# Pacing of attention and projections in the first layer: ratio 2.3 from a running base, without a lead

## The chip, the cores and the metric

The kernel runs on one core of a Trainium2 chip. The metric is the device time of one launch in microseconds (us); the time before is the median of three runs. The profiled execution is a further run with the hardware profiler on; its rows name the engines PE (TensorE matmul), PEld (TensorE weight load, overlapping PE), DVE (VectorE), ACT (ScalarE), POOL (GpSimd) and SP (SyncE, which issues the DMAs).

## The reference

A trunk of two layers on 1024 tokens of width 1024; each computes `x <- x + W_out(mixer(RMSNorm(x)) * silu(z))`. Layer 1 is a native sparse attention and is not touched by the change. Layer 0 is forgetting attention with 16 heads of 64:

```python
q, k, v, f, z = split(h @ w_in)
c = cumsum(log_sigmoid(f + b_f), axis=1)
logits = q @ k.T * HEAD_DIM ** -0.5 + c[query] - c[key]     # causal
o = softmax(logits) @ v
return (o * silu(z)) @ w_out
```

## The kernel before

**Two streams and a merge.** Layer 0 is written as two generators whose instructions are laid into one order by the function `merge`. `fox_main` is the attention, `fox_fill` the filling work, above all projections. Each generator yields the cost of what it has just emitted (a number, in the planner's nanoseconds), or a function that must become true before it goes on. `merge` takes one payment after another from `main`, adds it to `paid`, and after each lets `fill` run until `done`, the sum of the filling work, reaches `base + ratio * (paid + off)`. If `main` gives a function that isn't true yet, `fill` runs alone until it is. If `fill` itself gives such a function, fill is refused and attention goes on without it. A scheduler then places the instructions on the engines' queues, by priority in the written order; each engine runs its queue in order.

**The filling work.** For each of the 8 pairs of heads: `fox_k`, `fox_v`, `fox_q`, `fox_z`, each two halves of 512 tokens, each half 8 steps of three 128x512 matmuls (`project` through `mm3`, lines 132 to 134, cost 650 a step). `fox_k` of pair p >= 2 waits until pair p-2 is scored, `fox_v` until its products are done (the K and V tiles have two sets). Weights come by DMA into one staging tile (`load_w`, line 124), are cast on DVE (line 127), and POOL subtracts the cast for the low part (line 128). In pair 7, `load_wout` brings the output weights in two halves (ACT casts, line 525, POOL subtracts, line 526, eight each per half). After pair 7 comes `out_start`: products of the output projection for token tiles 4, 5 and 6. For tiles 4 and 5 the first four of their eight row blocks (16 steps) need pairs 0 to 3 only; the next three (12 steps) need pair 6; tile 6 (14 steps) waits until all scores are emitted.

**The attention.** A `FoxDuo` is two query tiles of one head: duo p.j.x is pair p (0 to 7), head j (0, 1) of the pair, x (0 to 3); there are 64. `score` makes the bias block `Bd` on POOL (line 563), multiplies queries with keys (lines 574 and 575) into one of three PSUM banks `S`, adds the bias and takes the running minimum on DVE (line 583), the exponential on ACT (line 592), splits the result into high and low half-precision parts (`hl`, ACT line 593, DVE line 594), and SP issues transposing DMAs into `pT` (line 595). `pv`, emitted two duos later, multiplies by V into a PSUM bank `O` (lines 608 and 609); `finish` reads it back on DVE (`ot`, line 620, and `o`, line 622). At the end of a pair the outputs are transposed (`pto`, line 630) and stored. `fox_main` emits the score of duo n, a payment, then the products of duo n-2, a second payment. The costs are `2 * max(n * 0.42, 107)` for each block of n columns scored and `85 * nk` for the products over nk key tiles. Eight duos before the end `fox_main` yields the tuple `(LAST,)`, by which `merge` sets the ratio anew and starts `paid` and `base` from that point.

**PSUM.** The banks `A` (three) hold projections, `O` and, from `out_start` on, output products.

Of the kernel before, what the change touches and what calls it, by code (L numbers as in the profile page):

```python
# [39 lines left out]
def tile_fox_nsa(ctx, tc, a, out):  # L40
# [156 lines left out]
    def merge(main, fill, ratio, off=0.0, until=None, rebase=False):  # L197

        done, paid, base = 0.0, 0.0, None

        def step():
            if blocked:
                if not blocked[0]():
                    return None
                blocked.pop()
            try:
                c = next(fill)
            except StopIteration:  # L210
                return None
            if callable(c):
                blocked.append(c)
                return 0.0
            return c

        for c in main:
            if callable(c):
                while not c():
                    n = step()  # L220
                    assert n is not None
                    done += n
                continue
            if isinstance(c, tuple):
                ratio, off, paid, base = c[0], 0.0, 0.0, done
                continue
            if base is None:
                base = done
            if rebase:
                base = max(base, done - ratio * (paid + off))  # L230
            paid += c
            while done < base + ratio * (paid + off):
                n = step()
                if n is None:
                    break
                done += n
        while not (until and until()) and step() is not None:
            pass
# [17 lines left out]
    def next_w(take=True):  # L256
        while len(wq) < 2 and fox_order:
            wq.append(wsec(*fox_order.pop(0)))
        return wq.pop(0) if take else None
# [53 lines left out]
    def fox_k(p):  # L313
        KH = [sa.tile([P, S], F32R, tag="KH", bufs=4, name=f"KH_{p}_{j}") for j in range(2)]
        KL = [sa.tile([P, S], F32R, tag="KL", bufs=4, name=f"KL_{p}_{j}") for j in range(2)]
        w = next_w() if p else wq.pop(0)
        for half in range(2):
            ts = slice(half * 512, half * 512 + 512)
            pt = ps_a(f"k{p}_{half}")
            yield from project(w, hT, half, pt)  # L320
            for j in range(2):
                r, o = rows[j], rows[1 - j]
                A.copy(KH[j][r, ts], pt[r, :])
                V.tensor_tensor(KL[j][r, ts], pt[r, :], f(KH[j][r, ts]), OP.subtract)
                dma(f(KH[j][o, ts]), f(KH[j][r, ts]))
                dma(f(KL[j][o, ts]), f(KL[j][r, ts]))
            yield 0
        ready["k", p] = KH, KL
# [57 lines left out]
    def fox_v(p):  # L386


        w = next_w()
        v = sa.tile([P, 2, 2, 4, P], F16, tag="v", bufs=2, name=f"v_{p}")  # L390
        sc = sa.tile([P, 4], F32, tag="vsc", bufs=3, name=f"vsc_{p}")
        vT = []
        for half in range(2):
            pt = ps_a(f"v{p}_{half}")
            yield from project(w, hT, half, pt)
            vT.append(f(sa.tile([P, 512], F32R, tag="Q", bufs=8, name=f"vT_{p}_{half}")))
            A.activation(vT[half], pt, AF.Abs, accum_out=sc[:, half:half + 1])
            A.copy(vT[half], pt)
        V.tensor_scalar(sc[:, 0:1], sc[:, 0:1], sc[:, 1:2], 2.0 ** -100, OP.max, OP.max)
        e, r = (sc[:, i:i + 1].bitcast(I32) for i in (2, 3))  # L400
        V.tensor_scalar(e, sc[:, 0:1].bitcast(I32), 0x7F800000, None, OP.bitwise_and)
        V.tensor_scalar(r, e, 0x7F800000, None, OP.bitwise_xor)
        V.tensor_scalar(sc[:, 3:4], sc[:, 3:4], 2.0 ** 13, None, OP.mult)
        V.tensor_scalar(sc[:, 2:3], sc[:, 2:3], 2.0 ** -15 / UP, None, OP.mult)
        for half in range(2):
            vs = sa.tile([P, 2, 512], F16, tag="vs", bufs=2, name=f"vs_{p}_{half}")
            A.activation(vs[:, 0], vT[half], AF.Copy, scale=sc[:, 3:4])
            V.scalar_tensor_tensor(vs[:, 1], vT[half], sc[:, 3:4], vs[:, 0], OP.mult, OP.subtract)
            nc.sync.dma_start_transpose(v[:, half].rearrange("p c t d -> p (c t) d"), vs.rearrange("p c t -> p (c t)"))
        ready["v", p] = v, sc[:, 2:3]  # L410

    def fox_q(p, w, halves=(1, 0)):
        Q = ready.setdefault(("qt", p), {})
        for half in halves:
            pt = ps_a(f"q{p}_{half}")
            yield from project(w, hT, half, pt)
            for j in range(2):
                Q[half, j] = q = sa.tile([P, 512], F32R, tag="Q", bufs=8, name=f"Q_{p}_{half}_{j}")
                r, o = rows[j], rows[1 - j]
                A.activation(q[r, :], pt[r, :], AF.Copy, scale=-SCALE)  # L420
                V.scalar_tensor_tensor(q[o, :], pt[r, :], -SCALE, f(q[r, :]), OP.mult, OP.subtract)
            ready["q", p, half] = Q

    def fox_z(p, w, halves=(1, 0)):
        zs = ready.setdefault(("zt", p), {})
        for half in halves:
            pt = ps_a(f"z{p}_{half}")
            yield from project(w, hT, half, pt)
            zs[half] = z = sb[0].tile([P, 512], F32, tag="z", bufs=4, name=f"z_{p}_{half}")
            silu2(z, pt)  # L430
            ready["z", p, half] = zs

    def fox_fill():
        for p in range(8):
            if p >= 2:
                yield lambda p=p: ("scored", p - 2) in ready
            yield from k0 if p == 0 else fox_k(p)
            if p == 0:
                for _ in range(11):
                    yield next(gate0)  # L440
            if p >= 2:
                yield lambda p=p: ("done", p - 2) in ready
            yield from fox_v(p)
            if p == 0:
                yield from gate0
                sb.append(tc.alloc_tile_pool(name="sb", bufs=2, reuse_waits="tile"))
            wo_copy(0, p)
            if p < 7:
                yield from fox_q(p, next_w())
                yield from fox_z(p, next_w())  # L450
            else:
                wq, wz = next_w(), next_w()
                for half in (1, 0):
                    yield from fox_q(p, wq, (half,))
                    yield from fox_z(p, wz, (half,))
                    yield from load_wout(hp, 0, half)
        yield from out_start()
# [55 lines left out]
    def wo_copy(i, k):  # L513
        dma(wD[i][k * P:(k + 1) * P, :], a[("fox_w_out", "nsa_w_out")[i]][k * P:(k + 1) * P, :])

    def load_wout(pool, i, half):

        hi, lo = (pool.tile([P, 4, D], F32R, tag=f"h{half}{x}", name=f"wo{i}_{half}_{x}") for x in range(2))
        for k in range(4):
            r = 4 * (1 - half) + k  # L520
            dma(f(lo[:, k, :]), wD[i][r * P:(r + 1) * P, :])
        for k in range(4):
            for c in range(2):
                cs = slice(c * 512, c * 512 + 512)
                A.copy(hi[:, k, cs], f(lo[:, k, cs]))
                G.tensor_tensor(lo[:, k, cs], f(lo[:, k, cs]), f(hi[:, k, cs]), OP.subtract)  # L526
            yield 200
        ready.setdefault("wout", []).append((hi, lo))


    PACE, LAST = 2.6, 2.6

    class FoxDuo:

# [113 lines left out]
    def fox_main():  # L648
        duos = [FoxDuo(p, j, x) for p in range(8) for j in range(2) for x in range(4)]
        for n in range(len(duos) + 2):  # L650
            if n == len(duos) - 8:
                yield (LAST,)
            if n < len(duos):
                yield from burst(duos[n].score(u) for u in (1, 0))
                if duos[n].j == 1 and duos[n].x == 3:
                    ready["scored", duos[n].p] = True
                    if duos[n].p == 7:
                        ready["scores"] = True
            if n >= 2:
                yield from burst(duos[n - 2].pv(u) for u in (0, 1))  # L660
                yield from duos[n - 2].finish()

    merge(fox_main(), fox_fill(), PACE, 5000)
    sb[0].release()
    sa.release()

# [725 lines left out]
```

## Time and profile before

| | |
|---|---|
| median of three runs | 1571.32 us (1570.53 to 1571.86) |
| the profiled execution | 1573.4 us, its span 1571.6 us |
| mean granted TensorE clock | 0.983 |
| PE / DVE / ACT / POOL busy | 95% / 71% / 56% / 35% of the span |
| layer 0's two streams | about 71 us to about 606 us |

The span runs from the first to the last instruction that the profile shows. Matmuls are pipelined and their ends are modelled, so a busy PE is not PE at its peak. In a row of the timeline the bracket gives the idle time of the engine just before the instruction and what released it. The granted clock is a mean over a stretch: 1.00 is TensorE's full 2.4 GHz, 0.50 the lower level of 1.2 GHz.

### The profile page before, as it was taken

How to read it: one execution, taken by the hardware profiler on the slowest of the kernel's cores; microseconds unless marked ns; L12 is line 12 of the kernel's file. 1: busy time of each engine (PE TensorE's matmuls, PEld its weight loads, DVE VectorE, ACT ScalarE, POOL GpSimd, SP SyncE). 2: the span in 40 equal slices, each digit the busy share in tenths (PEclk: the TensorE clock that was granted, in tenths of full speed). 3: DMA queues.
4: the chain of work that ended last, by engine and by line, in shares of the span. 5: the costliest groups of instructions: out<-in, count | busy, mean ns of one | idle time of the engine just before them, and what ended most of it. 6: DMA issues, size and time to landing. Idle time of an engine off the chain costs nothing.

```text
span 1571.6 us, 26098 instructions
## 1 busy us (share of the span) xinstructions
PE 1488.9 (95%) x8536; PEld 1245.3 (79%) x8536; DVE 1110.7 (71%) x2880; ACT 873.6 (56%) x2145; POOL 555.6 (35%) x596
## 2 busy tenths in 40 slices
PE   6999999999999787999999989999999999999898
PEld 4888888888777566878888777788888888888786
DVE  6568878788686855456464776888888888887433
ACT  5455655555555643233133544777787788787522
POOL 1222222232223400034242232546555556556400
PEclk9999999999999878999999999999999999999999
DMA  7777787777677756332436555502312312212452
GB/s 259 234 144 163 161 165 150 165 161 160 148 153 171 165 119 208 115 119 90 141 120 186 188 188 174 188 28 82 122 53 69 122 41 68 75 55 81 141 161 94
DMA packets 253945, 213.14 MB, mean 136 GB/s; under 512 B 179632, under 2 KB 201008, under 8 KB 253552
## 3 DMA queue, kind: packets, MB, share of 16 engines
q1 hardware_dynamic: 253808, 211.46, 49.2%
q8 instruction: 68, 1.11, 0.3%
q14 instruction: 69, 0.57, 0.1%
HBM read 123.06 MB, written 46.20 MB: 108 GB/s over the span
## 4 chain that ended last, share of the span: by engine, by line
PE 52%; DVE 12%; ACT 7%; DMA 4%; issue 4%; POOL 1%; SPq 0%; POOLq 0%; DVEq 0%; ACTq 0%
PE ptp_n L1250 7%; PE S_n L1226 7%; PE O_n L1259 3%; PE O_n L1258 3%; PE y L134 3%; PE y L133 3%; PE y L132 3%; ACT cP L1033 2%; DVE hl L594 2%; ACT P L592 1%; PE nz L132 1%; PE nz L133 1%; PE nz L134 1%; DMA wo<-wD 1%; ACT P_n L1234 1%
## 5 line engine op out<-in xcount | busy, mean ns | idle before, releaser
L1238 POOL TENSOR_SCALAR P_n<-P_n,l_n,gates 128x640 f32<-128x640 f32 (+7 forms) x256 | 200.9, 791 | 176.2 <-DVE l_n L1236 143.5
L145 DVE TENSOR_TENSOR ptl_n<-ptp_n,pth_n 128x512 fp32r<-128x512 f32 (+1 forms) x272 | 181.3, 672 | 35.3 <-ACT pth_n L144 31.6
L1234 ACT ACTIVATE P_n<-P_n,m_n 128x640 f32<-128x640 f32 (+7 forms) x256 | 188.5, 737 | 23.8 <-DVE m_n L1233 22.0
L144 ACT CAST pth_n<-ptp_n 128x512 fp32r<-128x512 f32 (+1 forms) x272 | 153.7, 568 | 73.5 <-PE ptp_n L1250 72.1
L592 ACT ACTIVATE P<-P,m 128x512 f32<-128x512 f32 (+1 forms) x192 | 116.8, 609 | 126.6 <-DVE m L583 125.9
L1226 PE MATMUL S_n<-nk,nq 128*128 128x320 f32 (+5 forms) x768 | 171.7, 333 | 0.2 <-DVE m_n L1233 0.2
L1250 PE MATMUL ptp_n<-ident,P_n 128*128 128x128 f32 x1056 | 166.9, 275 | 4.6 <-DVE ptl_n L145 2.9
L563 POOL TENSOR_TENSOR Bd<-B,tri 128x128 f32<-128x128 f32 x128 | 61.4, 491 | 250.6 <-DVE m L583 237.3
L1250 PEld LDWEIGHTS ptp_n<-ident,P_n 128*128 128x128 f32 x1056 | 124.6, 140 | 30.9 <-DVE ptl_n L145 8.1
L1258 PE MATMUL O_n<-pth_n,nv 128*128 128x512 f32 (+3 forms) x384 | 140.1, 369 | 0.8 <-DVE ot_n L1269 0.3
L1226 PEld LDWEIGHTS S_n<-nk,nq 128*128 128x128 f32 x768 | 128.0, 188 | 15.3 <-DVE m_n L1233 1.9
L594 DVE SCALAR_TENSOR_TENSOR hl<-P,hl 128x512 f16<-128x512 f32 (+1 forms) x192 | 125.7, 670 | 19.5 <-ACT hl L593 18.1
L1259 PE MATMUL O_n<-ptl_n,nv 128*128 128x512 f32 (+3 forms) x384 | 120.7, 338 | 0.1
L1233 DVE CUSTOM_DVE_ANT_0 P_n<-S_n,wmask 128x128 f32<-128x128 f32 (+1 forms) x192 | 113.3, 591 | 9.0 <-PE S_n L1226 4.7
L132 PE MATMUL y<-wo,ohi 128*128 128x512 f32 x240 | 97.1, 405 | 8.7 <-ACT ohi L688 4.6
L133 PE MATMUL y<-wo,ohi 128*128 128x512 f32 x240 | 96.6, 403 | 3.7 <-POOL wo L526 3.7
L134 PE MATMUL y<-wo,olo 128*128 128x512 f32 x240 | 95.8, 401 | 2.0 <-DVE olo L468 1.4
L593 ACT ACTIVATE hl<-P 128x512 f16<-128x512 f32 (+1 forms) x192 | 92.7, 513 | 3.4 <-DMA pT<-hl 1.7
L1258 PEld LDWEIGHTS O_n<-pth_n,nv 128*128 128x128 f32 x384 | 72.6, 189 | 6.9 <-DVE ot_n L1269 1.3
L574 PE MATMUL S<-KH,Q 128*128 128x512 f32 (+1 forms) x192 | 68.7, 372 | 8.0 <-DVE m L583 7.8
L1259 PEld LDWEIGHTS O_n<-ptl_n,nv 128*128 128x128 f32 x384 | 73.0, 190 | 2.2 <-DVE ptl_n L145 0.3
L608 PE MATMUL O<-v,pT 128*128 128x128 f16 x576 | 61.8, 226 | 8.3 <-DVE ot L620 4.7
(361 smaller groups left out, 4030.1 us busy)
## 6 DMA issues: line engine op xcount, KB each, us to landing
nq<-qD SPq DMA_DIRECT2D x64, 256.0 KB
B<-cD SPq DMA_DIRECT2D x16, 512.0 KB
wo<-wD SPq DMA_DIRECT2D x16, 512.0 KB
nq<-qD SPq DMA_DIRECT2D x64, 128.0 KB
of<-oF SPq DMA_DIRECT2D x12, 512.0 KB
x<-in_x_dram SPq DMA_DIRECT2D x8, 512.0 KB
wst_k<-in_fox_w_dram SPq DMA_DIRECT2D x8, 512.0 KB
wst_v<-in_fox_w_dram SPq DMA_DIRECT2D x8, 512.0 KB
```

The source lines that it names most:

```text
L132: T.matmul(ps, wh, mh, start=first, stop=False, **kw)
L133: T.matmul(ps, wh, ml, start=False, stop=False, **kw)
L134: T.matmul(ps, wl, mh, start=False, stop=last, **kw)
L144: A.copy(hi[:, 0:n], pt[:, 0:n])
L145: V.tensor_tensor(lo[:, 0:n], pt[:, 0:n], f(hi[:, 0:n]), OP.subtract)
L594: V.scalar_tensor_tensor(lo[:, cs], L[:, 0:n], UP, hi[:, cs], OP.mult, OP.subtract)
L1226: T.matmul(ps[:, b, 0:w], self.q[x][:, qi * P:(qi + 1) * P], k[:, k0 + b * w:k0 + b * w + w], start=(x == 0), stop=(x == 1))
L1234: A.activation(L, L, AF.Exp, bias=m, scale=-1.0, accum_out=lr[:, 0, qi:qi + 1])
L1238: G.tensor_scalar(L, L, lr[:, 1, qi:qi + 1], gates[:, i, x:x + 1], OP.mult, OP.mult)
L1250: T.transpose(pt[:, (x + i) * P:(x + i + 1) * P], L[:, kb * P - k0:(kb + 1) * P - k0], ident)
L1258: T.matmul(po[:, d], v, hi[:, c], start=(b == i == 0), stop=False)
L1259: T.matmul(po[:, d], v, lo[:, c], start=False, stop=(b == len(self.blocks) - 1 and i == len(pieces) - 1))
```

## The change

`PACE` becomes 2.3. The call for layer 0 loses the offset of 5000 and passes `rebase=True`, a branch of `merge` that the call of layer 1 already uses: ahead of each payment `base` is raised to `done - ratio * (paid + off)` if it lies below, so filling work that is ahead, because it ran alone or because its last step overshot, is not taken back later. `LAST` stays 2.6. No instruction is added or removed; only their order changes.

```diff
-    PACE, LAST = 2.6, 2.6
+    PACE, LAST = 2.3, 2.6
...
-    merge(fox_main(), fox_fill(), PACE, 5000)
+    merge(fox_main(), fox_fill(), PACE, rebase=True)
```

The lines of `merge` that this concerns:

```python
            if base is None:
                base = done
            if rebase:
                base = max(base, done - ratio * (paid + off))
            paid += c
            while done < base + ratio * (paid + off):
```

## Rows read from the trace of the kernel before

**Rows 1.** The page: busy us of each engine, share of the span, instructions.

```profile
PE 1488.9 (95%) x8536; PEld 1245.3 (79%) x8536; DVE 1110.7 (71%) x2880; ACT 873.6 (56%) x2145; POOL 555.6 (35%) x596
```

**Rows 2.** Windows: stretch, its length, PE, PEld, DVE, ACT, POOL busy, clock, DMA share, GB/s.

```profile
72.20:507.00 434.80, 428.40 (x2667) 351.75 (x2666) 333.63 (x996) 244.03 (x611) 127.05 (x144) 0.99 0.74 158
320.00:340.00 20.00, 20.00 (x134) 16.43 (x134) 18.20 (x54) 12.29 (x34) 6.53 (x8) 1.00 0.81 172
531.00:554.00 23.00, 14.46 (x112) 10.21 (x108) 19.25 (x70) 14.43 (x40) 4.24 (x9) 0.85 0.73 155
```

**Rows 3.** Timeline of PE in the opening: start, us, engine, line, output<-inputs.

```profile
72.24 0.40 PE L133 MATMUL z<-hT,whi_z 128*128 128x512 f32 x1
...
88.35 0.34 PE L574 MATMUL S<-KH,Q 128*128 128x384 f32 x1
...
95.92 0.23 PE L608 MATMUL O<-v,pT 128*128 128x128 f16 x1
```

**Rows 4.** Timeline of PE around the duos 4.1.3 and 5.0.1.

```profile
380.23 0.31 PE L574 MATMUL S<-KH,Q 128*128 128x128 f32 x1
...
381.47 0.23 PE L608 MATMUL O<-v,pT 128*128 128x128 f16 x1
...
383.18 0.50 PE L132 MATMUL k<-hT,whi_k 128*128 128x512 f32 x1 [0.77 <-DVE ot L620]
...
400.67 0.62 PE L132 MATMUL v<-hT,whi_v 128*128 128x512 f32 x1 [2.47 <-DVE ot L620]
```

**Rows 5.** Windows of DVE, lines 583, 594, 620, 622 in turn (34 duos).

```profile
100.00:369.00 269.00, 65.52 (x304) 1.00 0.77 163
...
100.00:369.00 269.00, 66.48 (x102) 1.00 0.77 163
...
100.00:369.00 269.00, 13.66 (x33) 1.00 0.77 163
...
100.00:369.00 269.00, 10.78 (x34) 1.00 0.77 163
```

**Rows 6.** Windows of 5 us at the gaps, all engines.

```profile
400.00:405.00 5.00, 4.33 (x12) 3.43 (x13) 4.65 (x18) 2.29 (x6) 0.88 (x2) 0.66 0.77 167
445.00:450.00 5.00, 2.54 (x24) 1.57 (x24) 4.83 (x18) 1.88 (x6) 0.91 (x2) 0.87 0.61 118
450.00:455.00 5.00, 5.00 (x32) 4.04 (x33) 4.23 (x11) 3.00 (x9) 3.57 (x3) 0.79 0.18 37
530.00:535.00 5.00, 2.23 (x25) 1.53 (x24) 3.08 (x10) 2.56 (x6) 1.20 (x3) 0.90 0.82 189
535.00:540.00 5.00, 4.40 (x29) 3.63 (x29) 3.80 (x17) 2.50 (x7) 0.87 (x2) 0.50 0.66 125
```

**Rows 7.** Timeline of PE around the duos 5.1.2 and 5.1.3, rows with idle time.

```profile
447.64 0.30 PE L574 MATMUL S<-KH,Q 128*128 128x128 f32 x1 [1.68 <-DVE m L583]
448.58 0.67 PE L574 MATMUL S<-KH,Q 128*128 128x512 f32 x1 [0.54 <-DVE m L583]
449.93 0.29 PE L608 MATMUL O<-v,pT 128*128 128x128 f16 x1 [0.25 <-DMA pT<-hl]
```

**Rows 8.** Timeline of PE after the score of duo 7.0.0 began.

```profile
535.39 0.27 PE L608 MATMUL O<-v,pT 128*128 128x128 f16 x1 [3.16 <-DVE ot L620]
```

**Rows 9.** Timeline of SP's queue: transposing DMAs of duo 0.0.0 and of 5.1.1.

```profile
76.04 3.97 SPq L595 DMA_TRANSPOSE pT<-hl  x2
...
443.96 3.55 SPq L595 DMA_TRANSPOSE pT<-hl  x2
```

**Rows 10.** Timeline of POOL and DVE: a weight subtract and a low half.

```profile
97.66 2.41 POOL L128 TENSOR_TENSOR wlo_q<-wst_q,whi_q 128x1024 fp32r<-128x1024 f32 x1 [2.01 <-PE O L609]
...
97.89 2.59 DVE L594 SCALAR_TENSOR_TENSOR hl<-P,hl 128x384 f16<-128x384 f32 x1
```

**Rows 11.** Windows of POOL, line 526 alone: the output weights' second half.

```profile
518.00:531.00 13.00, 11.07 (x8) 1.00 0.66 143
```

## The prediction

> **What bounds the kernel now.** I read the page first. TensorE is busy 95% of the span, VectorE 71%, ScalarE 56% [rows 1]: the time is TensorE's work plus the moments in which it has none, or has its slower clock. Next I cut the span into the stages around the edited `merge`. From 72.2 us (the first score ends there) to 507 us TensorE is busy 428.4 of 434.8 us; from 531 to 554 us, in the last pair of heads, only 14.5 of 23 us at a mean granted clock of 0.85 [rows 2]. The change adds and removes no instruction, so it can gain only what is lost to idle time and slow clock in layer 0, and can lose only by making new gaps. So I asked the timeline of TensorE for every gap, and set beside it what `merge` emits at that place.
>
> **How the order comes about.** `merge` is arithmetic and can be followed with a pencil. A duo pays `main` two sums: its score, 2 x 0.42 per column over 1152 columns = 968 (1074 for x = 0 and 3, where a block of 128 counts 107), and its products, 85 x 9 = 765. A step of filling work costs 650. A pair of heads has four projections of two halves of eight steps, 64 steps in all; its eight duos and the two yields of 1450 at its end pay 8167 + 6120 + 2900 = 17187.
>
> Before: 2.6 x 17187 = 44686, or 68.7 steps for 64 there are, and 5000 x 2.6 = 13000 (20 steps) on top as a lead. Fill is ahead from the start, and then meets its own guards: the keys of pair p wait for "scored" of p-2, its values for "done" of p-2. Followed through, fill is refused at duo 3.1.3 (pair.head.x), around 4.0.1, at 4.1.2 and 4.1.3, 5.0.0 and 5.0.1, 5.1.2 and 5.1.3, 6.0.0 and 6.0.1, and for nearly all of pair 7. When pair 7 begins, all of the first 16 product steps of `out_start` are already emitted.
>
> The trace bears the walk out. It puts 25 steps between the first two scores; the scheduler moved the first score one and a third steps down, and the remaining 23.67 steps take from 72.24 to 88.35 us, 0.68 us a step [rows 3]. So the scheduler keeps the written order to within a step or two. Where the walk has duo 4.1.3 with no fill, the score at 380.23 is followed by products at 381.47 and an idle gap [rows 4].
>
> After: ratio 2.3, no lead, and with `rebase` every payment starts from what has been done, so the overshoot of the last step is forgiven. 968 x 2.3 = 2226 rounds up to 4 steps, 765 x 2.3 = 1760 to 3: seven steps a duo, where before gave 4505 to 4782, on average 4644 / 650 = 7.1. **The rate is thus almost the same; the written 2.3 acts like 2.6.** What differs is the lead, gone, and the 17 steps that run alone before duo 1.0.0 (its queries come late now), not taken back later. Followed through, fill and attention run level to duo 5.1.3: refused are two steps there and three at 6.0.1, nothing else before the last pair. There 7 of the 16 product steps are emitted when pair 7 begins; the other 9 fall around duo 7.0.0. From 7.0.1 on both orders are the same. The LAST tuple stays; its ratio of 2.6 meets a fill that is refused until "scores", so it changes nothing.
>
> **The sum, part by part.**
>
> 1. *Duos without fill in pairs 4 to 6.* With 7 steps a duo takes TensorE 7 x 0.68 + 1.24 (score) + 0.94 (products) = 6.9 us [rows 3, 4]. VectorE needs (65.5 + 66.5 + 13.7 + 10.8) / 34 = 4.6 us for it [rows 5] and hides. Without fill TensorE has 2.2 us and waits. Loss at 4.1.3 and 5.0.1: gaps 0.77 + 2.47, then 5 us at a clock of 0.66, 0.34 x 5 = 1.7: 4.9 us [rows 4, 6]. Loss at 5.1.2 and 5.1.3: gaps 1.68 + 0.54 + 0.25, clock (0.13 + 0.21) x 5 = 1.7: 4.2 us [rows 6, 7]. Together 9.1 us. In the new order these duos have their seven steps. From below: nothing comes back if the waits are for PSUM and not for fill (a rival); from above 9.1. I take 9.1, because the duos that have fill at 320 to 340 us keep TensorE busy for all of the 20 us [rows 2].
>
> 2. *The last pair.* Nine steps (6.1 us of work done anyway) move to duo 7.0.0, which had none. Today TensorE sits 3.16 us before the products at 535.39, and its clock is 0.90 and 0.50 in the two slices there, (0.10 + 0.50) x 5 = 3.0 us [rows 6, 8]. From below, VectorE's need less TensorE's work: 4.6 - 2.2 = 2.4 us; from above 6.2. I take the gap alone, 3.2: the slow clock is likely to come one duo later. TensorE's waits for the split halves of the first output products stay: loads and splits still stand right ahead of them.
>
> 3. *The opening.* The first products now follow the first score by three stretches of 4 steps and two scores: 72.24 + 12 x 0.68 + 2 x 1.24 = 82.9 us, instead of 95.92 [rows 3, 4]. SP ends the issue of that duo's two transposing DMAs at 76.04 + 3.97 = 80.0 [rows 9]. The only case where the products wait for the landing is 449.93 [rows 7], 2.4 us after SP's issues begun at 443.96 had ended (447.51) [rows 9], so 82.4: half a microsecond to spare. Against it, duo 1's reduces now fall between duo 0's steps on VectorE: 65.5 / 34 = 1.9 us [rows 5]; queued behind them are duo 0's low halves, its transposes on SP, then its products. From below 0 (the scheduler may put `z` steps in front, and fill is plentiful), from above 1.9 for the reduces, 1.9 for one slow low half (2.59 against 0.65, rival A), and 1.7 for the clock: 5.5. I take 1.5. The 17 steps run alone cost TensorE nothing; VectorE and ScalarE have less to do meanwhile, and the ready products of pair 0 stand behind.
>
> 4. *The refused steps at 5.1.3 and 6.0.1* are a third of a duo each. At the nearest place, the refusals of three steps at 3.1.3 and of four or five around 4.0.1 (320 to 340 us), TensorE was never idle [rows 2]; the refusals of part 1, of a whole duo and more, cost some 4.5 each. I take 0.5.
>
> Costed at nothing: weight loads, casts and POOL subtracts keep their order among the steps and their rate of one per 16 steps; if that cover went, the next late thing would be a weight load behind SP's transposes.
>
> Sum: -9.1 - 3.2 + 1.5 + 0.5 = -10.3 us. The profiled execution took 1573.4 us (span 1571.6), 2.1 above the median of 1571.3; 1573.4 - 10.3 = 1563.1, and on the median's scale **1561.0 us**.
>
> **Rivals.**
> A. *The opening stalls.* Duo 0's chain loses the race of part 3, in full: 5.5 instead of 1.5 us, and once more for duo 1, whose products also come early: -10.3 + 4.0 + 4.0 gives 1569 us at worst, about 1566 with one. For it: the low half at 97.89 took 2.59 us, starting under a POOL weight subtract of 2.41 us that had begun at 97.66 [rows 10]; its kind takes 66.5 / 102 = 0.65 on average [rows 5]. Against: before's steady duos have the same seven steps and stall nowhere. The Trainium skill, "SBUF — State Buffer", section "SBUF: two separate sides", has it that VectorE with two SBUF inputs and GpSimd take an exclusive lock and the loser fully blocks. The trace agrees at that one place; by that rule alone, each low half of the opening that meets a subtract would come up to 2.4 us later.
>
> B. *The gaps are PSUM waits and return.* Both gaps at 383.18 and 400.67 are put down to `ot` [rows 4], the read that frees an attention bank, and every pair ends that way. Then only the place changes: 1571, within 3. Against: pair 3 ends the same way at 320 to 340 us, with fill, and has no such gap [rows 2].
>
> C. *Slower: the second half of the output weights.* It is emitted right before the 16 product steps, two duos later than today. Its eight POOL subtracts keep POOL busy 11.1 of 13 us at 518 to 531 [rows 11], and the bias block `Bd` of each score queues behind them on POOL; VectorE's minimum waits for that, then TensorE for the bank. If this meets 7.0.0 and 7.0.1, each may cost what 7.0.0 costs now, 6.2 us. It decides once the two lose more than the 9.1 of part 1 and the 3 us that can be told from no change: -9.1 + 12.4 + 2.0 (parts 3 and 4) = +5.3, or 1577 us. For it: those duos have no fill in the end. Against: the 9 steps at 7.0.0 give `Bd` some 6 us more before TensorE needs the bank.
>
> D. *The change does not reach the engine*, because the scheduler reorders by readiness. The walk and the trace agree too well for more than a small chance; 1571 us.
>
> **How the numbers follow.** Forecast 0.60 (its own range 1554 to 1566), A 0.16, B and D 0.13, C 0.11. About 3 us, 0.2%, is what a measurement of this kernel can tell from no change. A still ends below 1568 in nearly all of its chance, so faster 0.77, same 0.13, slower 0.10. Best case, all of part 2 and no cost: 1571.3 - 15.3 = 1556, and a few us less if the later gaps shrink too: 1553. The range reaches from there to 1571, which leaves out C and the upper half of B and D.
>
> **What would show it.** Right: the second score some 3 to 4 us after the first; no TensorE gap above 0.5 us from 100 us to duo 5.1.3 and a granted clock of 1.00 there; product steps between the scores of 7.0.0 and 7.0.1; the end of layer 0 about 10 us earlier; every later stage unchanged. Part 3 is wrong if a gap before the first products names the transposing DMA; part 1 if `ot` ends gaps at pair ends that have fill; part 2 if the idle before 7.0.1's products has grown to what 7.0.0's was. The prediction fails as a whole if the last pair becomes longer than pairs 4 to 6 become shorter.

## The result and the profile after

The changed kernel takes 1560.61 us (median of 4 runs, 1557.2 to 1560.89) against 1571.59 us (1570.53 to 1572.4, 4 runs) of the kernel before beside it: a ratio of 0.9926, 95% interval 0.9908 to 0.9943. That is faster by about 11 us, where 1561.0 was forecast. The profiled execution has a span of 1559.1 us at a mean granted clock of 0.986; before, 1571.6 and 0.983.

The page, busy time of each engine, beside [rows 1]:

```profile
PE 1483.0 (95%) x8536; PEld 1242.4 (80%) x8536; DVE 1111.3 (71%) x2880; ACT 873.2 (56%) x2145; POOL 558.0 (36%) x596
```

Counts of instructions are the same to the last one; TensorE is busy 5.9 us less for the same matmuls, which goes with the higher mean clock, and its idle time is 6.6 us less. The windows that answer to [rows 2], and the 20-us windows around the places of [rows 6]:

```profile
72.30:507.00 434.70, 430.98 (x2722) 354.22 (x2721) 344.31 (x1028) 250.08 (x626) 130.75 (x147) 1.00 0.76 162
320.00:340.00 20.00, 20.00 (x122) 16.51 (x121) 16.93 (x45) 9.96 (x27) 4.97 (x6) 1.00 0.74 162
531.00:554.00 23.00, 19.23 (x120) 15.12 (x118) 16.39 (x58) 12.36 (x32) 3.14 (x7) 0.85 0.77 150
...
400.00:420.00 20.00, 20.00 (x124) 16.51 (x123) 14.70 (x43) 9.65 (x24) 7.07 (x6) 1.00 0.73 169
440.00:460.00 20.00, 20.00 (x135) 16.46 (x135) 17.44 (x53) 12.30 (x34) 5.10 (x7) 1.00 0.71 163
```

Up to 507 us TensorE does 55 matmuls more than before in the same time, and at 400 to 420 and 440 to 460 us, where before had its gaps and the clock of [rows 6], it is busy all the time at 1.00. What TensorE waits for from 72 to 500 us (what waits, on what, us in total, times, longest), before:

```profile
PE S L574 <- DVE m L583: 2.9, 5, 1.7
PE v L132 <- DVE ot L620: 2.5, 1, 2.5
PE k L132 <- DVE ot L620: 0.8, 1, 0.8
PE O L608 <- DMA pT<-hl: 0.2, 1, 0.2
```

and after:

```profile
PE pto L630 <- DVE o L622: 0.9, 1, 0.9
PE S L574 <- DVE m L583: 0.2, 1, 0.2
PE v L132 <- DVE KL L324: 0.2, 1, 0.2
```

The opening of the changed kernel, timeline of PE, beside [rows 3]:

```profile
72.29 0.48 PE L574 MATMUL S<-KH,Q 128*128 128x512 f32 x1
...
75.36 0.34 PE L574 MATMUL S<-KH,Q 128*128 128x384 f32 x1
...
80.07 0.50 PE L574 MATMUL S<-KH,Q 128*128 128x512 f32 x1 [0.17 <-DVE m L583]
...
83.36 0.23 PE L608 MATMUL O<-v,pT 128*128 128x128 f16 x1
```

From the start of the first score to that of the second it is 3.1 us (before 17.4, 71.0 to 88.35), the first products come at 83.36 us (82.9 forecast), and the one gap is 0.17 us.

In the last pair the idle time moved and did not go. Timeline of PE after the last projections, rows with idle time:

```profile
506.21 0.30 PE L574 MATMUL S<-KH,Q 128*128 128x128 f32 x1 [1.76 <-DVE m L583]
...
508.03 0.51 PE L574 MATMUL S<-KH,Q 128*128 128x512 f32 x1 [0.84 <-DVE m L583]
...
521.39 0.80 PE L574 MATMUL S<-KH,Q 128*128 128x512 f32 x1 [3.69 <-DVE m L583]
...
537.61 0.50 PE L574 MATMUL S<-KH,Q 128*128 128x512 f32 x1 [1.27 <-DVE m L583]
...
540.94 0.29 PE L608 MATMUL O<-v,pT 128*128 128x128 f16 x1 [1.02 <-DMA pT<-hl]
```

The 3.16 us of [rows 8] are gone, and a gap of 3.69 us stands in the middle of the 16 product steps instead. The timeline of all engines shows what is behind it:

```profile
515.20 0.08 DVE L583 DVE_READ_ACCUMULATOR2_ANT m<- 128x1 f32 x1
...
516.04 1.14 ACT L525 CAST wo<-wo 128x512 fp32r<-128x512 f32 x2 [3.17 <-DMA wo<-wD]
...
517.08 0.72 ACT L592 ACTIVATE P<-P,m 128x512 f32<-128x512 f32 x1
...
518.63 0.63 DVE L617 TENSOR_TENSOR l<-l 128x1 f32<-128x1 f32 x1 [2.69 <-ACT P L592]
...
519.55 2.16 ACT L525 CAST wo<-wo 128x512 fp32r<-128x512 f32 x4
```

ScalarE stood 3.17 us before a cast of the output weights whose DMA had not landed. The exponential at 517.08 is queued behind it, VectorE's sum at 518.63 waited 2.69 us for the exponential, and the minimum that frees the score's bank comes behind that. The minimum which this exponential needs had been read out at 515.28 (515.20 + 0.08): the queue held it back by 1.8 us, not by the whole 3.17. So by this chain the late DMA accounts for about half of the 3.69 us; the rest is the exponential, the split and the minimum themselves.

The balance in the profiled executions: the first score starts 1.3 us later than before; up to there TensorE has the same 249 instructions in both, and in the other runs that have them too the start lies between 71.2 and 72.4 us, so this is spread between runs. From the first score to the end of the last output product of tile 6 it is 518.6 us (72.3 to 590.9), before 530.8 (71.0 to 601.8): 12.2 us less. What comes behind is 1.6 us shorter (968.2 for 969.8): its order is the same and its gaps nearly so, but from 20 to 40 us behind that end the granted clock is 0.91 against 0.83, 0.08 x 20 = 1.6 us. -12.2 - 1.6 + 1.3 makes the 12.5 us between the spans.

### The profile page after: what moved, and what is told of

It reads as the page before. It is cut to its first block, busy times and chain, and to the rows that moved or that the text cites. A ratio compares the mean times of both kernels' runs of the same rounds, so it can differ in the third digit from the quotient of the medians.

```text
span 1559.1 us, 26094 instructions
## 1 busy us (share of the span) xinstructions
PE 1483.0 (95%) x8536; PEld 1242.4 (80%) x8536; DVE 1111.3 (71%) x2880; ACT 873.2 (56%) x2145; POOL 558.0 (36%) x596
## 4 chain that ended last, share of the span: by engine, by line
PE 72%; DVE 12%; ACT 7%; DMA 4%; issue 3%; POOL 1%; SPq 0%; POOLq 0%; DVEq 0%; ACTq 0%
PE ptp_n L1250 7%; PE S_n L1226 7%; PE O_n L1259 3%; PE y L134 3%; PE O_n L1258 3%; PE y L133 3%; PE y L132 3%; PE v L132 2%; PE v L134 2%; PE v L133 2%; PE S L574 2%; PE S L575 2%; PE O L608 2%; PE k L132 2%; PE q L132 2%
## 5 line engine op out<-in xcount | busy, mean ns | idle before, releaser
L144 ACT CAST pth_n<-ptp_n 128x512 fp32r<-128x512 f32 (+1 forms) x272 | 153.8, 569 | 73.6 <-PE ptp_n L1250 72.3
L1233 DVE CUSTOM_DVE_ANT_0 P_n<-S_n,bias 128x640 f32<-128x640 f32 (+1 forms) x64 | 64.9, 1016 | 4.6 <-PE ptp_n L1250 3.7
```

The lines of the kernel that those rows point to most:

```text
L144: A.copy(hi[:, 0:n], pt[:, 0:n])
L1233: V.tensor_tensor_reduce(dst, src, mk, 1.0, 3e38, OP.add, OP.min, m)
```

## The experiments

All kernels compute the whole reference; only the order of the instructions differs. A ratio is against the kernel before, run beside it on the same chip, 5 rounds, with its 95% interval. "Steps a duo" are from following `merge` with a pencil, as in the prediction.

**1. The changed kernel with the lead put back.**

```diff
-    merge(fox_main(), fox_fill(), PACE, rebase=True)
+    merge(fox_main(), fox_fill(), PACE, 5000, rebase=True)
```

> The changed kernel with the lead alone put back: ratio 2.3, offset 5000, rebase kept. Followed through, fill is then refused for a whole duo at 5.1.3 and for nine steps around 6.0.1, and all but seven of the first 16 output products stand ahead of pair 7 again to within a step or two. Theory (what costs is a duo without fill, 2.4 to 6 us each; the lead makes such duos): one and a half such duos in pairs 5 and 6 and one in pair 7 come back, 1567 us (1564 to 1571). Rival (what helps is that forced work is forgiven; a lead is harmless): 1560.6 within 2.

Measured: 1562.67 us, 0.9923 (0.9911 to 0.9935), the same as the change. From 72 to 500 us TensorE waits 1.3 + 1.0 + 0.2 us in all. With the lead the scores of 5.1.3 and of 6.0.1 have no fill behind them, each by itself: the first cost 0.95 us, the second nothing. The lead as such isn't what cost the 9.1 us of the prediction's part 1; my theory missed here.

**2. The kernel before, only without its lead.**

```diff
-    merge(fox_main(), fox_fill(), PACE, 5000)
+    merge(fox_main(), fox_fill(), PACE)
```

> The kernel before with the lead alone taken out: ratio 2.6, no offset, no rebase. The 17 steps that run alone before duo 1.0.0 are then taken back: duos 1.0.0, 1.0.1 and 2.0.0 get no fill, pairs 3 to 6 run level, and pair 7 has 28 product steps on its first two and a half duos. Theory (count of duos without fill): two and a half are lost early, 6 to 9 us against the changed kernel, about two are gained in pair 7, 5 to 8 us: 1562 us (1557 to 1567). Rival (forgiving forced work is what brings the gain): no better than 1568 to 1572.

Measured: 1558.1 us, 0.9897 (0.9884 to 0.991). Neither the ratio of 2.3 nor the running base is needed for the gain. Duo 1.0.0 and the beginning of 1.0.1 have no fill here, right after a stretch of lone steps; at 120 to 140 us TensorE is still busy 19.90 of 20 us. Its one wait above 0.4 us up to 500 us is another: 2.28 us at 316.08, for the queries of pair 4 (`Q`, line 421).

**3. The changed kernel at the old ratio.**

```diff
-    PACE, LAST = 2.3, 2.6
+    PACE, LAST = 2.6, 2.6
```

> The changed kernel with the ratio written as 2.6 instead of 2.3. With every payment rounded up to whole steps a duo then gets 8 or 9 steps instead of 7. Followed through, fill runs ahead of its guards from pair 2 on, and some 26 duos between 2.1.2 and 6.1.3 have none. Theory (rounding: 2.3 acts like 2.6, so 2.6 acts like 3.0): 26 duos at 2.4 to 4.2 us each, 1625 us (1600 to 1670). Rival (the written ratio is the rate; 2.6 is the rate of the kernel before, whose loss was the lead): 1558 to 1566.

Measured: 1603.98 us, 1.019 (1.0176 to 1.0204): slower by 30 us than before. TensorE's waits from 72 to 540 us:

```profile
PE S L574 <- DVE m L583: 9.9, 8, 3.2
PE O L608 <- DMA pT<-hl: 8.2, 6, 2.7
PE v L132 <- DVE ot L620: 1.7, 1, 1.7
```

With every overshoot forgiven 2.6 acts like 3.0 or more, 8 to 9 steps a duo, and 26 duos have no step, or a single one, between their score and the products behind it. The direction is what the rounding says, and the total lies in the range; a duo costs less than the 2.4 to 4.2 us expected: the 41 us between this and experiment 1 are 1.6 us for each of the 26, on average and with all that differs put down to them.

**4. The changed kernel with 2.0 for both ratios.**

```diff
-    PACE, LAST = 2.3, 2.6
+    PACE, LAST = 2.0, 2.0
```

> The changed kernel with both ratios at 2.0: six steps a duo instead of seven. No refusal up to pair 7; nine of the steps of pair 7's projections run alone ahead of it, and it has fill up to duo 7.0.3 instead of 7.0.0. Theory (a duo without fill costs 3 to 4 us, and six steps still hide VectorE: 2.2 + 6 x 0.68 = 6.3 us of TensorE work a duo): three such duos fewer, 1550 us (1546 to 1555). Rival (the last pair is held by the output weights on POOL and by PSUM banks, not by missing fill): 1559 to 1563. Rival (six steps are too few for VectorE): above 1563, with new gaps in pairs 1 to 6.

Measured: 1580.17 us, 1.0033 (1.0021 to 1.0045). The forecast and the first rival missed. The second rival has the time and the new gaps, but not their reason, which is a wait that none of the three had. TensorE's waits, 72 to 500 us, and then the timeline of all engines at the beginning of pair 2:

```profile
PE S L574 <- DVE Q L421: 19.1, 5, 4.0
```

```profile
191.92 3.43 DVE L594 SCALAR_TENSOR_TENSOR hl<-P,hl 128x512 f16<-128x512 f32 x2
...
195.38 0.68 DVE L421 SCALAR_TENSOR_TENSOR Q<-q,Q 64x512 fp32r<-64x512 f32 x1
...
196.12 0.50 PE L574 MATMUL S<-KH,Q 128*128 128x512 f32 x1 [3.62 <-DVE Q L421]
```

By the walk 2.0 gives 4 + 3 steps to the duos x = 0 and 3, 3 + 3 to x = 1 and 2 (not six to all, as the expectation had it) and 12 at the end of a pair: 64, just what a pair has. So the queries of a pair are finished just as its first score is due. VectorE's part of them (line 421) stands behind two low halves that take 3.43 us. The first of the two took 0.68; the second, at 192.53, took 2.83, under a weight subtract that POOL ran from 192.14 to 194.81. TensorE waits so at each of pairs 2 to 6. In the changed kernel, at seven steps, fill gains some four steps on attention in each pair, and the queries lie ready.

**5. The same, with older queries.** The first score of a pair now also asks for the gate's first half, so eight more steps come between the queries and the score.

```diff
-    PACE, LAST = 2.3, 2.6
+    PACE, LAST = 2.0, 2.0
...
-            yield lambda: ("q", p, 1) in ready and ("q", p, 0) in ready
+            yield lambda: ("q", p, 0) in ready and ("z", p, 1) in ready
```

> Both ratios 2.0 as in the run before it that came out slower, and a pair's first score now also waits, in the written order, until the first half of its z projection is emitted, so its queries are eight steps old. Theory (at 2.0 the first score of pairs 2 to 6 waits 3.6 to 4.0 us for VectorE's second query part, which stands behind low halves slowed by a POOL weight subtract): these waits and the half clock after them go, some 30 us, and the fuller last pair's 8 us show: ratio to the kernel before 0.987 (0.984 to 0.990). Rival (six steps a duo are too few to hide VectorE): 1.000 or above, with waits moved to other scores.

Measured: 1554.21 us, 0.9877 (0.986 to 0.9894): 1.6 points below experiment 4, and from 72 to 500 us the only wait listed is 0.5 us for `ot`. The query wait was the cause.

**6. A rate of 1.6, and fill for the whole last pair.** Ratios 1.6 and 1.4; in pair 7 all queries come first, then gate and output weights by halves.

```diff
-    PACE, LAST = 2.3, 2.6
+    PACE, LAST = 1.6, 1.4
...
+                yield from fox_q(p, wq)
                 for half in (1, 0):
-                    yield from fox_q(p, wq, (half,))
                     yield from fox_z(p, wz, (half,))
```

> Ratio 1.6 up to pair 7 (five steps a duo; some 15 steps of each pair run alone ahead of it), 1.4 in pair 7, whose queries are both projected ahead of its z: then every duo of pair 7 has five steps. Theory (what costs is a wait of VectorE's chain, and steps that run alone let VectorE drain, so the first score doesn't wait; five steps give TensorE 2.2 + 3.4 = 5.6 us a duo against 4.6 of VectorE): the last pair loses little, ratio 0.985 (0.980 to 0.990). Rival (five steps are too few, because the projections' own VectorE work comes on top): gaps of about 1 us in each of 48 duos, ratio 1.01 or above.

Measured: 1547.56 us, 0.9838 (0.9822 to 0.9854), the fastest of all. Five steps a duo keep TensorE nearly as busy as seven (waits of 5.3 us from 72 to 500 us, 1.3 in the change), and by the walk every duo of the last pair has its five too.

**7. The last pair of 6 at the old rate without lead.** Ratios 2.6 and 1.4, no lead, no running base, the order of pair 7 as in 6.

> The kernel before without lead and without rebase (2.6; measured at 0.990 before), with both query halves of pair 7 ahead of its z, and the ratio 1.4 in pair 7, so that its 28 product steps spread over duos 7.0.0 to 7.1.1 at three a duo. Theory (a duo without fill costs most when several follow each other): 0.987 (0.983 to 0.990). Rival (pair 7 is held by the output weights, on ScalarE, POOL and DMA): 0.990 within 0.001.

Measured: 1556.51 us, 0.9886 (0.9869 to 0.9903). This doesn't tell the two apart.

**8. The changed kernel with late casts.** The DMAs of the output weights' second half stay in place; its casts and subtracts are written only after the first 16 product steps.

```diff
-                    yield from load_wout(hp, 0, half)
-        yield from out_start()
+                    cast = load_wout(hp, 0, half)
+                    yield next(cast)
+                    if half:
+                        yield from cast
+        yield from out_start(cast)
...
             yield from products(t, slice(0, 4))
+        yield from cast
...
             dma(f(lo[:, k, :]), wD[i][r * P:(r + 1) * P, :])
+        yield 0
```

> The changed kernel, with the ScalarE casts and POOL subtracts of the second half of the output weights emitted after the first 16 product steps; their DMAs stay where they are. Theory (the 3.69 us wait ahead of the second part of duo 7.0.0's score comes because exponentials stand behind casts on ScalarE that wait for the weights' DMA): that wait goes, 3 to 5 us, ratio 0.990 (0.988 to 0.9915). Rival (the score waits for its PSUM bank through POOL's bias block, or through VectorE's load): 0.9926 within 0.0015.

Measured: 1558.87 us, 0.9906 (0.989 to 0.9921): in time not told apart from the change. The timeline of ScalarE, then that of PE:

```profile
514.50 1.14 ACT L530 CAST wo<-wo 128x512 fp32r<-128x512 f32 x2 [0.74 <-DMA wo<-wD]
515.54 0.72 ACT L597 ACTIVATE P<-P,m 128x512 f32<-128x512 f32 x1
```

```profile
508.62 0.50 PE L132 MATMUL y<-wo,ohi 128*128 128x512 f32 x1 [4.60 <-DVE Q L421]
...
520.29 0.51 PE L579 MATMUL S<-KH,Q 128*128 128x512 f32 x1 [0.95 <-DVE m L588]
```

The new written order did not reach ScalarE. On its queue the order from 495 us until behind the score's gap is that of the changed kernel: the first two casts still stand ahead of the same exponential, and seven of the eight begin (514.50 to 521.98) before the last of the 16 product steps has (525.9). So the run doesn't test the theory. What it shows is that the two waits are short together: ScalarE stands 0.74 us before the cast and not 3.17, and TensorE's gap is 0.95 us and not 3.69. Of these 2.7 us, 1.1 are a bank that comes free earlier (the score at 520.29 for 521.39), and 1.6 a TensorE that comes to it later (at 519.34 for 517.70). For ahead of the first output product there is now a wait of 4.60 us, put down to line 421, which reads the last queries out of their bank, where the change has 1.76 + 0.84: 2.0 us more.

**9. The kernel before with the ratio 2.3 alone;** the lead stays, no running base.

```diff
-    PACE, LAST = 2.6, 2.6
+    PACE, LAST = 2.3, 2.6
```

> The kernel before with the ratio 2.3 alone: the lead of 5000 stays and nothing is rebased. Without the rounding in its favour 2.3 gives 6.1 steps a duo, so the lead shrinks by some three steps a pair; from pair 2 on the queries of the next pair are asked for before they are there, 5 to 16 steps run alone, and the next duo, at most two, has none. By what the runs without lead showed, such a pair of duos costs 1 us or less (VectorE has caught up during the lone steps), and the last pair keeps fill to its end: 0.990 of the kernel before (0.985 to 0.994). Rival: with a rate of 2.3 the running base is what makes the gain, and the lone steps taken back cost 4 to 5 us at each of five pair ends: 0.998 or more.

Measured: 1552.53 us, 0.9871 (0.9854 to 0.9889), more than the whole change brings. Windows of its last pair, and those of the change after them:

```profile
500.00:520.00 20.00, 19.08 (x116) 14.99 (x114) 11.09 (x31) 11.74 (x25) 12.24 (x10) 1.00 0.45 142
520.00:540.00 20.00, 16.35 (x113) 12.17 (x114) 18.55 (x56) 14.45 (x36) 12.30 (x15) 1.00 1.04 236
540.00:560.00 20.00, 18.19 (x104) 14.32 (x103) 15.28 (x50) 11.81 (x32) 4.79 (x5) 0.91 0.57 113
560.00:580.00 20.00, 18.33 (x126) 14.41 (x124) 5.98 (x17) 3.26 (x9) 0.00 (x0) 1.00 0.37 85
```

```profile
500.00:520.00 20.00, 14.50 (x83) 10.49 (x81) 15.35 (x43) 14.62 (x35) 13.06 (x13) 0.90 0.82 199
520.00:540.00 20.00, 15.79 (x104) 12.29 (x104) 15.57 (x50) 11.05 (x30) 10.90 (x13) 0.84 0.70 147
540.00:560.00 20.00, 16.75 (x104) 13.36 (x104) 13.04 (x45) 10.66 (x28) 2.25 (x5) 0.83 0.64 133
560.00:580.00 20.00, 15.54 (x85) 12.08 (x85) 10.79 (x42) 9.01 (x25) 0.46 (x1) 0.83 0.54 105
```

Idle time in these 80 us is 8.1 against 17.4 us, and the clock is 0.91 to 1.00 against 0.83 to 0.90. At 6.1 steps a duo fill is left for the last six duos by the walk; the change has none from 7.0.2 to 7.1.2. The gain comes in spite of a loss: from 72.2 to 300 us TensorE is idle for 7.9 us, before for 0.5, and more than half of it is the query wait of experiment 4, once, at the first score of pair 1 (timeline of PE):

```profile
137.44 0.79 PE L574 MATMUL S<-KH,Q 128*128 128x512 f32 x1 [4.47 <-DVE Q L421]
```

**10. The changed kernel at 2.1.**

```diff
-    PACE, LAST = 2.3, 2.6
+    PACE, LAST = 2.1, 2.6
```

> The changed kernel with 2.1 for 2.3. Rounding theory: 968 x 2.1 still rounds up to four steps and 765 x 2.1 to three, so the order is the same up to pair 5 and the time that of the changed kernel: 0.9926 (0.991 to 0.9945). Rival: the written rate counts in proportion, and 2.1 lies two thirds of the way to the 2.0 that cost 1.07 points: 0.998 to 1.001, with the first score of a pair waiting for its queries.

Measured: 1558.93 us, 0.9914 (0.9899 to 0.9929): the time of the change. Its waits from 72 to 500 us are the change's too (0.9 for `o`, 0.2 for `KL`, no query). Between 2.1 and 2.3 the time does not change, and at 2.0, where the score payment of the duos x = 1 and 2 drops from four steps to three, the query wait begins: the rounding sets the rate, as the prediction had it.

**11. Ratios 1.6 and 1.4 with the old order in pair 7.**

> The ratios 1.6 and 1.4 with the last pair's projections in the order of the kernel before (queries of the second half, gate of the second half, weights, and only then queries of the first half). Theory: the fill of the last pair is then asked for in one lone stretch of 29 steps ahead of duo 7.0.0 and is used up four duos before the end; these four come without fill, as they do in the changed kernel: 0.987 (0.985 to 0.9895). Rival: the rate alone made the gain of the 1.6 and 1.4 kernel: 0.9838 within 0.0015.

Measured: 1553.35 us, 0.988 (0.9862 to 0.9897). The queries' place in pair 7 is worth 0.4 points: without it 22 steps of the pair's queries and gate are forced to run alone ahead of duo 7.0.0 (14 in experiment 6), and toward the end duo 7.1.2 has no fill. The time is as expected, the way there only in part: by the walk one duo is left without fill, and not four. The gain of experiment 6 is thus that of the rate and of this order together.

**12. The changed kernel without its running base:** ratio 2.3, no lead, lone steps taken back.

```diff
-    merge(fox_main(), fox_fill(), PACE, rebase=True)
+    merge(fox_main(), fox_fill(), PACE)
```

> The changed kernel without its running base: 2.3, no lead, lone steps taken back. Per pair 17 to 41 steps run alone, and then 1.6 duos (pair 1) growing to 4.7 duos (pair 7) have none, some 20 in all. Theory (the first one or two after a lone stretch are free, since VectorE has caught up, and each further one costs 1.5 to 4 us; the last three duos keep fill, which gives some 10 us back): 1.008 of the kernel before (0.996 to 1.02). Rival: after lone steps unfilled duos are free in any number, and the last pair is better filled: 0.985.

Measured: 1565.27 us, 0.9951 (0.9937 to 0.9966), between the two. TensorE's longest waits, 72 to 500 us:

```profile
PE O L608 <- DMA pT<-hl: 10.8, 13, 2.4
PE S L574 <- DVE m L583: 2.9, 6, 0.7
```

In these 428 us TensorE is idle for 18.1 and its clock is 0.97 from 300 us on. Duos without fill are not free in any number after lone steps: the products wait for the transposing DMA, the last link of their own chain.

## Why the prediction was right

**The total** came out at 1560.6 for 1561.0; its own range (1554 to 1566) holds it. The profiled span fell by 12.5 us where the sum said 10.3. That the medians meet within 0.4 us is luck in part: parts 1, 3 and 4 gave 0.9 us more than the sum has for them and part 2 gave 1.0 more, the 1.6 us of clock behind layer 0's streams stand in no part ("every later stage unchanged" was wrong there), and a start that was 1.3 us later took some of it back.

**Parts 1, 3 and 4.** The last projection ends 432.2 us after the first score (504.5 - 72.3), before 437.1 (508.1 - 71.0), and by the walk one score and the products of two duos more are done by then, 1.24 + 2 x 0.94 = 3.1 us. So 8.0 us came back, where the three parts together gave 9.1 - 1.5 - 0.5 = 7.1. The waits for `ot` and `m` in pairs 4 and 5 are gone, and the two slices of slow clock with them. Rival B, that these were PSUM waits which would return, is refuted by the waits after. Parts 3 and 4 were too dear: the opening cost 0.17 us for 1.5, and in all of 380 to 500 us, where the refused steps are, TensorE is idle 0.3 us. That leaves 8.2 of part 1's 9.1. One sign was missed: a gap above 0.5 us does stand between 100 us and duo 5.1.3, 0.90 at 210.76, where the outputs of a pair are transposed.

**What the gaps of part 1 were made of.** The prediction read them as VectorE's 4.6 us against TensorE's 2.2. At the first two places there is more to it. The timelines of VectorE and POOL, kernel before:

```profile
380.40 2.38 POOL L128 TENSOR_TENSOR wlo_v<-wst_v,whi_v 128x1024 fp32r<-128x1024 f32 x1 [1.32 <-PE O L609]
380.77 2.02 DVE L617 TENSOR_TENSOR l<-l 128x1 f32<-128x1 f32 x1 [0.51 <-ACT P L592]
382.71 0.41 DVE L620 TENSOR_REDUCE ot<-O 128x128 f32<-128x256 f32 x1
...
397.39 2.35 POOL L128 TENSOR_TENSOR wlo_q<-wst_q,whi_q 128x1024 fp32r<-128x1024 f32 x1 [2.73 <-PE S L575]
397.88 2.40 DVE L594 SCALAR_TENSOR_TENSOR hl<-P,hl 128x512 f16<-128x512 f32 x1
...
400.20 0.41 DVE L620 TENSOR_REDUCE ot<-O 128x128 f32<-128x256 f32 x1
```

Right ahead of each `ot` that TensorE waited for (gaps of 0.77 and 2.47 us) VectorE had an instruction stretched under a POOL weight subtract: 2.02 us for one that takes 0.16 at other places, 2.40 us for a low half that takes 0.65 on average [rows 5]. The excess, 1.9 and 1.75 us, is more than the first gap and most of the second. This is the mechanism of rival A, where the prediction didn't look for it. In the changed kernel such stretched instructions are as many (16 of more than 0.8 us excess from 72 to 500 us, before 15), for example 2.45 us at 460.36, but fill stands behind the scores there and TensorE doesn't wait. So missing fill laid a delay of VectorE bare; the forecast that fill removes the gaps holds for either reading. At 5.1.2 and 5.1.3 there is no subtract, and there the prediction's reading stands. No run moves the subtracts by themselves.

**Part 2** is the remainder, 12.2 - 8.0 = 4.2 us for 3.2. But it isn't the simple removal of one gap: TensorE lost 3.69 us at 521.39 to a new one. That is rival C's place (output weights right ahead of the 16 product steps) by another link than C named: the casts on ScalarE, held by their DMA, and not the subtracts on POOL; by that chain they account for about half of it (1.8 us). It cost one gap instead of two of 6.2 us, so C did not decide. Why the last pair gained 4.2 us is not shown: experiment 8, which was to test it, did not move the casts.

**Rival A** fell: no products in the opening waited for a transpose. (Its milder sum is added up wrongly: -10.3 + 4.0 gives 1565 us, not 1566.) **Rival D** fell: the order reached the engine as the walk had it.

**What was too simple.** The prediction put the 9.1 us down to the lead. That fits its rows, but experiments 1, 2 and 9 correct it: with the lead and the running base there is no loss; without the lead alone the loss is gone too; and with the lead and 2.3 it is gone as well. Nor does a duo without fill have one price: 0.95 us or nothing in experiment 1, 1 us or less for two behind lone steps (experiment 2; in the kernel before 6.0.0 and 6.0.1, behind 16 steps of fill in a row, cost nothing), 1.6 us for each of 26 (experiment 3), 4.2 us for 5.1.2 and 5.1.3 in succession, and 0.8 and 4.2 us for 4.1.3 and 5.0.1, each by itself but behind a stretched VectorE instruction. And the prediction asked only what 2.3 does to pairs 1 to 6, where seven steps and 7.1 are indeed the same; it did not ask what a lower rate would leave for pair 7, where the larger reserve lay (experiments 6 and 9).

**Open.** Whether the change is slower than its single parts is shown for the ratio alone (experiment 9, intervals apart: 0.9854 to 0.9889 against 0.9908 to 0.9943), and not for the missing lead alone (0.9884 to 0.991). Whether the running base helps at 2.3 without a lead can't be said surely either: the profiled spans say 5 us (1559.1 against 1564.5), the intervals of the change and of experiment 12 touch. Experiment 10, which by the rounding has the same seven steps as the change, does lie apart from experiment 12, measured beside it (0.9899 to 0.9929 against 0.9937 to 0.9966). No run moved the casts on ScalarE's queue.

## What to carry to other kernels

Where filling work is laid between dependent chains by a ratio, first work out with the pencil how a payment rounds to whole steps and where fill is refused: the written ratio may act like another. Here 2.3 with the running base gave the steps of 2.6 without it, and 2.1 those of 2.3, while 2.0 did not. Then give each chain only as much fill as keeps the busy engine busy (here five steps did nearly what seven did) and save the rest for the stretch at the end where nothing else is left. When an operand is finished only just in time, look at what is queued ahead of its last step on the engine that finishes it.

## What the runs showed of the hardware

- Under a POOL weight subtract (128x1024, 2.66 us, from 192.14 to 194.81 in experiment 4) a low half on VectorE that began 0.39 us after it took 2.83 us and ended 0.54 us behind it, where one takes 0.65 on average [rows 5]; in the kernel before a sum of 128x1 elements took 2.02 us for 0.16. The Trainium skill, "SBUF — State Buffer", section "SBUF: two separate sides", says that the two engines lock each other out in such a pair; the trace agrees. In the prediction this was a danger for the opening, which it did not touch; it was part of 3.6 to 4.0 us in each of five pairs of experiment 4, where VectorE's next instruction was one that TensorE needed, and of the two `ot` gaps of the kernel before.
- After a TensorE gap of 3.62 us (experiment 4, ended at 196.12) the granted clock was 0.68 for the 5 us from 195 on, against 1.00 in the 15 us ahead: with 0.32 x 5 = 1.6 us of it, the gap cost some 5.2 us and not 3.6.
- A late DMA holds more than the instruction that needs it: in the changed kernel ScalarE stood 3.17 us before one cast, and an exponential behind it, whose minimum was there at 515.28, began at 517.08.
